# A hybrid decoder step (RWKV-7, RG-LRU, cross-attention): TensorE's order fixed by hand in the RWKV chain and the LRU stage, units reordered, keys scaled per token

## The chip, the core and the metric

The kernel runs on one core of one Trainium2 chip. The metric is the device time of one execution, in microseconds; less is better. The core has five engines with an instruction stream each: TensorE (PE; its weight loads are shown apart as PEld), VectorE (DVE), ScalarE (ACT), GpSimd (POOL) and SyncE (SP, which issues most DMAs). They wait for each other by semaphores, and each runs its own stream in order.

## The reference

One layer, for a prompt of 512 tokens and for 8 samples of 8 tokens (576 tokens in all), width 1024:

```python
xn = rmsnorm(x, g_norm)
u, za, xb, zb, q, zc, gates = split_in(xn @ w_in)      # 1024 x 11392
oa, ... = rwkv7_branch(u, za, ...)     # 16 heads of 64: s = s*w + sa (kk*a)^T + v k^T ; o = s r
ob, ... = rglru_branch(xb, zb, ...)    # conv of 4, two block gates, h = a*h + b
oc = cross_attn(q, zc, mem_k, mem_v)   # 4 heads of 256, 256 memory rows
g_a, g_b, g_c = split(sigmoid(gates))
merged = g_a * (oa @ w_br_a) + g_b * (ob @ w_br_b) + g_c * (oc @ w_br_c)
y = x + merged @ w_out                 # then a last rmsnorm
```

In the RWKV branch the key direction `kk` is normalized per token and head: `kk * rsqrt(sum(kk*kk) + eps)`. The samples bring states and memory keys and values of their own; the prompt starts from zero states and computes its keys and values (`kv`).

## The kernel before

**The stream.** All large projections are cut into units of 128 output columns (class `Stream`, `step` at line 330). Operands are split in two parts (`hi` and `lo`, type fp32r), so a step is three products (hi*xh, hi*xl, lo*xh), each in two halves of 288 tokens: six matmuls on the whole 128x128 array, all recorded at line 355. Eight steps make a unit. Its weights (512 KB) are fetched by SP, ScalarE makes `whi` (line 280) and VectorE makes `wlo` (line 281), one unit ahead; at the end of a unit the evacuation (`use`) is queued. `st.go(n)` writes n steps at that place of the program, `st.until(label)` all steps to the end of a unit. Units come from two lists: `first` (needed at a due place) and `fill` (spilled to DRAM until used). Names in the profile are those of the units: `u` (RWKV inputs), `za`, `zb`, `zc` (gates), `xb` (LRU input), `g` (merge gates), `q`, `kv`, `br` (branch outputs).

**Order.** The program is written with the stream's steps between the pieces of the branches. A scheduler then orders each engine's instructions by what is ready in its estimate, so single stream matmuls and small products are mixed more finely than they are written.

**Stages.** Start and norms (to 62 us), memory keys and values with attention (`attention`, line 660, to 223), RWKV (`rwkv_phase`, line 802, to 884), the last `zb` units (to 936), the LRU stage beside the projections `br2` and `br0` (`lru_phase`, line 468, to 1065), `br1` (to 1119), output projection and norm (`final`).

**An RWKV group.** Four groups of two pairs of heads (`o0`, `o1`), in chunks of 64 tokens; a ninth chunk holds the samples. `prep_a`, `prep_b`, `prep_c` make decays and keys; the products `m` (line 990) of keys and reads are masked and, on VectorE, multiplied by the reciprocal key norm `rsv`, which lies per partition there (`M`, line 996). The same factor goes into the transposed keys (`BKn`, line 981). `invert` (line 1000) sends 32x32 blocks of `M` through DRAM (`d<-M`, `X<-d`) and solves 72 unit triangles by substitution on VectorE (lines 1016, 1018); `invert2` (line 1035) fetches the result, and TensorE forms the other blocks: `z` (line 1041) and `w` (line 1050) on 32x32 tiles of the array, in two halves of nine, each result copied by ScalarE (lines 1045, 1054). `solved` (line 1082) then applies the inverses (`U`, `W` on 64x64 tiles). The chain (line 1123) goes over eight chunks; in each, `A` (line 1128, whole array) multiplies by the state `sbd`, VectorE adds it to `UV` (line 1121), then `dS` (line 1137) and `A` (line 1113) run on 128x64 tiles, and the new state is made by POOL (line 1130) and VectorE (line 1145). `sample_a`, `sample_b`, `sample_c` handle the samples' states inside the chain (`s0t`, `A8` at line 1189 on 128x32 tiles, `dSs`, `s1t`). The stream between these is what `st.go(2)` and `st.go(4)` put there.

**The LRU stage.** For each of eight column blocks: `conv` (ScalarE and VectorE), `gates` (products `pg`, line 516; tanh and exponentials on ScalarE; scaling by `c4` on VectorE, line 521), `scan` (POOL makes `be`, lines 543 and 544; VectorE scans at line 546 and multiplies by the gate), and `split` (line 590) into the operand of the last projections (`oh`, `ol`). The sum over branches (`merged`) is on POOL for the middle branch (line 452).

Of the kernel before, what the change touches and what calls it, by code (L numbers as in the profile page):

```python
# [18 lines left out]
P = 128  # L19
D = 1024  # L20
KC = 8
# [25 lines left out]
class Kern:  # L47
    def __init__(self, ctx, tc, ins, outs):
# [7 lines left out]
        self.dq = 0  # L56

# [4 lines left out]
    def transpose(self, out, in_, rows):  # L62

        self.nc.tensor.transpose(out, in_, self.ident[:rows, :rows])  # L64
# [151 lines left out]
    def softplus(self):  # L216
# [9 lines left out]
        nc.vector.tensor_scalar(self.c4, self.c4, -4.0, None, op0=ALU.mult)  # L226

# [77 lines left out]
class Stream:  # L305
# [24 lines left out]
    def step(self):  # L330
# [22 lines left out]
        for q, (a, b) in enumerate(((hi, xh), (hi, xl), (lo, xh))):  # L353
            for o, t0, m in parts:
                nc.tensor.matmul(self.ps[:, o:o + m], a[:, k, :], b[:, k, t0:t0 + m],  # L355
                                 start=(k == 0 and q == 0), stop=(k == KC - 1 and q == 2))
# [35 lines left out]
def spill_units(K, pool):  # L392
# [38 lines left out]
    us = [Unit(w, C_G + D * b + P * j, x, gate(K.gd[b, j]), f"g{b}{j}") for b in (2, 0, 1) for j in range(KC)]  # L431
    us += [Unit(w, C_ZC + P * j, x, silu2(K.ocz[j], K.ocd[j]), f"zc{j}") for j in range(KC)]
    us += [Unit(w, C_XB + P * j, x, conv_in(j), f"xb{j}") for j in range(KC)]
    us += [Unit(w, C_ZB + P * j, x, silu2(K.zbd[j]), f"zb{j}") for j in range(KC)]
    return us


def branch_units(K, pool, b, w, oh, ol, place, out=None):
# [3 lines left out]
    def mk(j):  # L442
        def use(pb):
# [7 lines left out]
            if place == "mid":  # L451
                nc.gpsimd.tensor_add(m, m, t)
# [15 lines left out]
def lru_phase(K, o2, then):  # L468
# [4 lines left out]
    with tc.tile_pool(name="lruc", bufs=1, reuse_waits="tile") as lc, tc.tile_pool(name="lru", bufs=2, reuse_waits="tile") as lp:  # L473
# [9 lines left out]
        ohl = []  # L483
# [21 lines left out]
        def gates(j):  # L505
            if j % 4 == 0:
                quad[j // 4] = lp.tile([P, 4, N], F32, tag="args", name="args")
# [3 lines left out]
            for q, bh in enumerate((K.bah, K.bxh)):  # L511
                g = lp.tile([P, N], F32, tag=f"g{q}", name=f"g{q}")
                for s in range(2):
                    pg = K.psb(f"pg{q}")[:, 0:HN]
                    cs = slice(HN * s, HN * s + HN)
                    nc.tensor.matmul(pg, wbd[q][:, j, :], xc[:, cs], start=True, stop=True)
# [3 lines left out]
            c4 = K.c4[:, j:j + 1]  # L520
            nc.vector.tensor_scalar(gr, gr, c4, c4, op0=ALU.mult, op1=ALU.add)
# [3 lines left out]
            nc.scalar.activation(ap_, gr[:, 0:TP], AF.Exp)  # L525
            nc.scalar.activation(as_[:, :, 1:9], smp(gr), AF.Exp)
            th = lp.tile([P, AE], F32, tag="th", name="th")[:, 0:N]
            nc.scalar.activation(th, gr, AF.Tanh, scale=-1.0)
            nc.scalar.activation(gr, gr, AF.Exp, scale=2.0)
            nc.vector.scalar_tensor_tensor(ar, gr, 1.0, th, op0=ALU.add, op1=ALU.mult)  # L530
            gx = lp.tile([P, N], F32, tag="gx", name="gx", bufs=4)
# [3 lines left out]
        def scan(j):  # L535
# [7 lines left out]
            nc.gpsimd.tensor_mul(bp_, ar[:, 0:TP], gx[:, 0:TP])  # L543
            nc.gpsimd.tensor_mul(bs_[:, :, 1:9], smp(ar), smp(gx))
# [5 lines left out]
            o = lp.tile([P, N], F32, tag="g0", name="lo")  # L550
            nc.vector.scalar_tensor_tensor(o[:, 0:TP], hp_, 0.5, z2[:, 0:TP], op0=ALU.mult, op1=ALU.mult)
# [956 lines left out]
```

## Time and profile before

| | |
|---|---|
| median of 3 runs | 1182.16 us (1181.98 to 1182.41) |
| the profiled execution | 1184.47 us |
| its span in the trace | 1182.7 us |
| mean granted TensorE clock | 0.992 |
| busy share PE, DVE, ACT, POOL | 97%, 60%, 44%, 16% |
| the chain that ended last | PE 79%, DVE 7%, ACT 5%, issue 3%, DMA 3%, POOL 2% |
| HBM | read 120.82 MB, written 29.01 MB, 127 GB/s over the span |

Matmuls overlap in the trace: a stream matmul is recorded with about 0.30 us, and the next one starts 0.13 us after it. So a busy share of TensorE says little about how close together its matmuls are; the chain in order of time, whose pieces are merged from start to start, says more. A row of the timeline merges neighbours of one kind (x2, x8); in square brackets stands idle time before it, and what ended it. A float32 product of the program appears as two records.

### The profile page before, as it was taken

The page shows a single profiled execution, that of the slowest core. Times are in us where ns is not written, and L with a number is a line of the kernel's source. Part 1 is how long each engine was busy: PE and PEld are TensorE (multiplying, and loading weights), DVE is VectorE, ACT ScalarE, POOL GpSimd, SP SyncE. Part 2 cuts the span into 40 slices and gives each one's busy share as a digit, 9 for nine tenths or more (in the row PEclk, how much of TensorE's full clock was granted, in tenths as well). Part 3 has the DMA queues.
Part 4 walks back from the last instruction along what each step waited for, and adds up shares of the span by engine and source line. Part 5 has one row for each costly group of instructions (what it writes and reads, how often), then busy time and mean ns, then how long its engine had stood idle before and what let it go on. Part 6 is the DMA issues. An engine that isn't in the chain of part 4 may idle for free.

```text
span 1182.7 us, 25731 instructions
## 1 busy us (share of the span) xinstructions
PE 1145.4 (97%) x10567; PEld 1068.8 (90%) x10567; DVE 713.2 (60%) x1436; ACT 517.3 (44%) x1004; POOL 184.3 (16%) x311
## 2 busy tenths in 40 slices
PE   6999999999999999999999999999999999979997
PEld 4998877899998898988989989999889999979997
DVE  5345655238764687835788457874455386975633
ACT  5444544337324374243752336532444266442333
POOL 3010001010003210022100130101211012570031
PEclk9999999999999999999999999999999999998999
DMA  4447685522452233532233522345337665348412
GB/s 140 130 145 233 211 254 189 162 81 66 107 140 73 65 93 82 142 89 70 78 92 120 145 73 65 106 125 149 85 90 232 203 195 170 104 115 261 117 45 81
DMA packets 220623, 151.50 MB, mean 128 GB/s; under 512 B 52640, under 2 KB 196106, under 8 KB 220506
## 3 DMA queue, kind: packets, MB, share of 16 engines
q1 hardware_dynamic: 217242, 146.87, 42.1%
q10 hardware_dynamic: 3264, 2.99, 0.9%
q8 instruction: 83, 1.36, 0.5%
q14 instruction: 34, 0.28, 0.1%
HBM read 120.82 MB, written 29.01 MB: 127 GB/s over the span
## 4 chain that ended last, share of the span: by engine, by line
PE 79%; DVE 7%; ACT 5%; issue 3%; DMA 3%; POOL 2%; SPq 0%; DVEq 0%; ACTq 0%; POOLq 0%
PE u L355 13%; PE g L355 12%; PE br L355 9%; PE xb L355 4%; PE zc L355 4%; PE za L355 4%; PE fo L1349 4%; PE q L355 4%; PE zb L355 3%; PE kv L355 2%; PE m L990 1%; PE dS L1137 1%; DVE wlo L281 1%; DMA wraw<-in_w_mem_kv 1%; PE skt L64 1%
## 5 line engine op out<-in xcount | busy, mean ns | idle before, releaser
L280 ACT CAST whi<-wraw 128x1024 fp32r<-128x1024 f32 x129 | 135.4, 1050 | 292.6 <-PE g L355 90.7
L281 DVE TENSOR_TENSOR wlo<-wraw,whi 128x1024 fp32r<-128x1024 f32 x128 | 158.9, 1241 | 127.5 <-ACT whi L280 126.7
L355 PE MATMUL u<-xh,whi 128*128 128x288 f32 x400 | 92.2, 305 | 0.0
L355 PE MATMUL br<-oh,wlo 128*128 128x288 f32 x384 | 84.4, 302 | 4.4 <-DVE wlo L281 4.3
L355 PE MATMUL u<-xl,whi 128*128 128x288 f32 x400 | 88.6, 300 | 0.0
L355 PE MATMUL u<-xh,wlo 128*128 128x288 f32 x400 | 88.6, 299 | 0.0
L355 PE MATMUL br<-oh,whi 128*128 128x288 f32 x384 | 85.4, 305 | 3.0 <-ACT oh L592 2.9
L355 PE MATMUL g<-xh,whi 128*128 128x288 f32 x384 | 86.6, 304 | 0.0
L355 PE MATMUL g<-xh,wlo 128*128 128x288 f32 x384 | 84.7, 300 | 0.0
L355 PE MATMUL g<-xl,whi 128*128 128x288 f32 x384 | 84.4, 301 | 0.0
L355 PE MATMUL br<-ol,whi 128*128 128x288 f32 x384 | 84.2, 301 | 0.0
L355 PEld LDWEIGHTS u<-xh,whi 128*128 128x128 f32 x400 | 65.1, 188 | 5.5 <-issue 4.1
L355 PEld LDWEIGHTS br<-oh,wlo 128*128 128x128 f32 x384 | 63.5, 194 | 5.6 <-DVE wlo L281 5.6
L355 PEld LDWEIGHTS br<-oh,whi 128*128 128x128 f32 x384 | 63.7, 193 | 4.3 <-ACT oh L592 3.4
L355 PEld LDWEIGHTS u<-xl,whi 128*128 128x128 f32 x400 | 64.7, 188 | 2.0 <-issue 1.4
L355 PEld LDWEIGHTS u<-xh,wlo 128*128 128x128 f32 x400 | 64.7, 188 | 0.9 <-issue 0.2
L355 PEld LDWEIGHTS g<-xh,whi 128*128 128x128 f32 x384 | 62.3, 190 | 3.2 <-issue 3.1
L355 PEld LDWEIGHTS g<-xh,wlo 128*128 128x128 f32 x384 | 62.7, 190 | 1.2 <-issue 1.2
L355 PEld LDWEIGHTS br<-ol,whi 128*128 128x128 f32 x384 | 63.4, 193 | 0.1
L355 PEld LDWEIGHTS g<-xl,whi 128*128 128x128 f32 x384 | 62.4, 190 | 1.1 <-issue 1.1
L1016 DVE TENSOR_TENSOR Xt<-X 72x30 f32<-72x30 f32 (+14 forms) x120 | 39.3, 328 | 11.4 <-DMA X<-d 7.8
L1349 PE MATMUL fo<-wol,oh 128*128 128x256 f32 (+1 forms) x160 | 45.0, 282 | 0.0
(386 smaller groups left out, 2894.3 us busy)
## 6 DMA issues: line engine op xcount, KB each, us to landing
wraw<-in_w_in SPq DMA_DIRECT2D x89, 512.0 KB
wraw<-in_w_mem_kv SPq DMA_DIRECT2D x16, 512.0 KB
kn<-in_cache_mem_k SPq DMA_DIRECT2D x16, 512.0 KB
kn<-in_cache_mem_v SPq DMA_DIRECT2D x16, 512.0 KB
gd<-flt SPq DMA_DIRECT2D x24, 288.0 KB
gtt<-gd SPq DMA_DIRECT2D x24, 288.0 KB
wraw<-in_w_br_c SPq DMA_DIRECT2D x8, 512.0 KB
wraw<-in_w_br_a SPq DMA_DIRECT2D x8, 512.0 KB
```

Source lines behind the costliest of these rows:

```text
L64: self.nc.tensor.transpose(out, in_, self.ident[:rows, :rows])
L280: nc.scalar.copy(hi, raw)
L281: eng.tensor_sub(lo, raw, hi.bitcast(F32))
L355: nc.tensor.matmul(self.ps[:, o:o + m], a[:, k, :], b[:, k, t0:t0 + m], start=(k == 0 and q == 0), stop=(k == KC - 1 and q == 2))
L990: nc.tensor.matmul(pms[h][64 * w:64 * w + 64, P * (c - c0):P * (c - c0) + P], BK[64 * h:64 * h + 64, c, w, :], ZR[64 * h:64 * h + 64, c].r ...
L1016: nc.vector.tensor_mul(tv, X[:, 0:s, s:s + 1].to_broadcast([NQ, s, m]), X[:, s:s + 1, s + 1:].to_broadcast([NQ, s, m]))
L1137: nc.tensor.matmul(pS[hs, C * o.q:C * o.q + C], o.BKn[:, c, hs], o.UV[:, c, hs], start=True, stop=True, tile_position=(0, 64 * h))
L1349: nc.tensor.matmul(pos[t][:r, :W], a[:, k, t * P:t * P + r], b[:, k, :], start=(k == 0 and q == 0), stop=(k == KC - 1 and q == 2))
```

## The change

It has six parts.

1. **Order fixed by hand.** All matmuls go through a helper `mm` (line 71 of the changed kernel), transposes through line 65. While `K.pin` is set, their order on TensorE is that of the program. It is set through the chain of each RWKV group and through the LRU stage. A chain step is now: A with the state, `s0t` or `s1t` if any, two stream steps (one in the last group), then `dS`, `A` and the samples' products on tiles, then four (three) stream steps.
2. **Inversion.** 38 in place of 37 steps before `invert2`, and the first M block is sent to DRAM per pair of heads as soon as it is made (`products`); `invert` only loads, `substitute` solves.
3. **Keys scaled by channel row, not by partition.** The reciprocal norms are made in `prep_a`, written to DRAM transposed (1152 elements of 4 bytes a pair), and read back to all partitions into `sq`. The keys are multiplied by it before the products, so that the mask is one multiplication for four chunks, and the transposed keys are plainly copied by ScalarE.
4. **Attention.** The samples' scores of the second group are written beside the values of the first (one PSUM bank, same 128x32 tiles), loads are issued close to their use, and more stream steps lie between.
5. **Fill order.** `zb`, 16 gates, `xb`, 4 gates, `zc`, and the last 4 gates, in place of gates, `zc`, `xb`, `zb`.
6. **LRU stage.** It starts when `zc7` is done, beside the last four gate units; the gate products are spread, scans of the first half come before the rest's gates, the operand `oh`/`ol` is made later; `c4` becomes scale and bias of ScalarE's activations; `be` and the middle sum of `merged` go from POOL to VectorE. The last states are written out after `br11`.

Cut to its core:

```diff
+    def mm(self, *a, **kw):
+
+        ins = self.nc.tensor.matmul(*a, **kw)
+        if self.pin:
+            self.tc.keep_in_program_order(ins)
+        return ins
...
-    us = [Unit(w, C_G + D * b + P * j, x, gate(K.gd[b, j]), f"g{b}{j}") for b in (2, 0, 1) for j in range(KC)]
...
+    return zb + g[:16] + xb + g[16:-4] + zc + g[-4:]
...
             if place == "mid":
-                nc.gpsimd.tensor_add(m, m, t)
+                nc.vector.tensor_add(m, m, t)
...
-            nc.vector.tensor_scalar(gr, gr, c4, c4, op0=ALU.mult, op1=ALU.add)
...
-            nc.scalar.activation(ap_, gr[:, 0:TP], AF.Exp)
+            nc.scalar.activation(ap_, gr[:, 0:TP], AF.Exp, scale=c4, bias=c4)
...
-            nc.gpsimd.tensor_mul(bp_, ar[:, 0:TP], gx[:, 0:TP])
-            nc.gpsimd.tensor_mul(bs_[:, :, 1:9], smp(ar), smp(gx))
+            nc.vector.tensor_mul(bp_, ar[:, 0:TP], gx[:, 0:TP])
+            nc.vector.tensor_mul(bs_[:, :, 1:9], smp(ar), smp(gx))
...
+        K.pin = True
+        conv(0)
+        st.go(8)
+        conv(1)
+        st.go(6)
+        gates(0)
+        conv(2)
+        st.go(5)
+        gates(1)
+        st.until("g17")
+        oa, then = merge()
...
+            rvf = rv.rearrange("p h c -> p (h c)")
+            nc.vector.reciprocal(rvf, rvf)
+            d4 = dr.tile([18, C], F32, tag="d4", name="d4")
+            nc.sync.dma_start(d4.rearrange("x t -> t x"), rvf)
+            d4h = d4.rearrange("(h c) t -> h (c t)", h=2)
+            for h in range(2):
+                nc.sync.dma_start(sq[64 * h:64 * h + 64, :], d4h[h:h + 1, :].to_broadcast([64, N]))
...
-            nc.vector.scalar_tensor_tensor(sq, ta, 1.0, zn, op0=ALU.add, op1=ALU.mult)
-            nc.vector.tensor_mul(BK[:, :, zs, :], chk(sq), chk(o.pinv))
+            nc.vector.tensor_mul(sq, sq, o.pinv)
+            nc.vector.scalar_tensor_tensor(BK[:, :, zs, :], chk(ta), 1.0, chk(zn), op0=ALU.add, op1=ALU.mult)
+            nc.vector.tensor_mul(BK[:, :, zs, :], BK[:, :, zs, :], chk(sq))
...
+                for h in range(2):
+                    nc.vector.tensor_mul(M1.rearrange("p (c h) m -> p c h m", h=2)[:, c0:c0 + n, h, :],
+                                         pms[h][:, 0:P * n].rearrange("p (c m) -> p c m", m=P),
+                                         maskq[q][c0 == 8].unsqueeze(1).to_broadcast([P, n, P]))
...
-            st.go(37)
+            st.go(38)
             invert2(prs)
...
+            K.pin = True
             for c in range(8):
-                chain(prs, c)
-                if c in (1, 4):
-                    sample_a(prs[c // 4])
-                if c in (2, 5):
-                    sample_b(prs[c // 4])
-                if c in (3, 6):
-                    sample_c(prs[c // 4])
+                chain(prs, c, (2, 4) if g + 1 < NG else (1, 3), fulls.get(c, none), tileds.get(c, none))
+            K.pin = False
```

On TensorE in a chain step of the first group, before (u are stream units, M the two pairs' products; x2 counts neighbours of one kind):

```order
L1128 MATMUL A<-sbd_2475,ZR 128x128 x2
L355 MATMUL u_4497<-xl,whi 128x288 x2
L355 MATMUL u_4497<-xh,wlo 128x288 x2
L1137 MATMUL dS<-UV,BKn 64x64 x2
L355 MATMUL u_4598<-xh,whi 128x288
L1137 MATMUL dS<-UV,BKn 64x64 x2
L1113 MATMUL A<-UV,M_3281 64x64
L1113 MATMUL A<-UV,M_3428 64x64
```

And in such a step of the changed kernel:

```order
L71 MATMUL A<-sbd_2645,ZR 128x128 x2
L71 MATMUL u_4443<-xh,whi 128x288 x2
L71 MATMUL u_4443<-xl,whi 128x288 x2
L71 MATMUL u_4443<-xh,wlo 128x288 x2
L71 MATMUL u_4443<-xh,whi 128x288 x2
L71 MATMUL u_4443<-xl,whi 128x288 x2
L71 MATMUL u_4443<-xh,wlo 128x288 x2
L71 MATMUL dS<-UV,BKn 64x64 x4
L71 MATMUL A<-UV,M_3412 64x64
L71 MATMUL A<-UV,M_3534 64x64
```

Twelve stream matmuls now stand between A with the state and dS, and none stands among the tile products.

On TensorE at the inversion of the first group, before (the first z, of the first pair, stands 13 rows of stream ahead of this):

```order
L355 MATMUL u_4256<-xl,whi 128x288 x2
L1041 MATMUL z_3972<-xz,M_3428 32x32 x9
L1050 MATMUL w_3993<-M_3281,xz 32x32 x9
L355 MATMUL u_4256<-xh,wlo 128x288 x2
L355 MATMUL u_4256<-xh,whi 128x288 x2
L355 MATMUL u_4256<-xl,whi 128x288 x2
```

And in the changed kernel:

```order
L71 MATMUL g_4091<-xh,wlo 128x288 x2
L71 MATMUL z_4149<-xz,M_3412 32x32 x9
L71 MATMUL z_4150<-xz,M_3534 32x32 x9
L71 MATMUL w_4171<-M_3412,xz 32x32 x9
L71 MATMUL w_4172<-M_3534,xz 32x32 x9
L71 MATMUL z_4193<-xz,M_3412 32x32
```

The stream matmuls between z and w have gone ahead of all of them; the two pairs' second z and w follow, and then U.

On VectorE near the end of the LRU stage, before (he is the scan, lo its gated result, ol the operand's low part, br a branch projection's result):

```order
L546 SCALAR_TENSOR_TENSOR he<-ae,be 128x584 x2
L593 TENSOR_TENSOR ol<-lo,oh 128x576
L450 SCALAR_TENSOR_TENSOR gtt<-gtt,br_12562 128x576
L551 SCALAR_TENSOR_TENSOR lo<-he,z_12649 128x512
L552 SCALAR_TENSOR_TENSOR lo<-he,z_12649 128x64
L551 SCALAR_TENSOR_TENSOR lo<-he,z_12704 128x512
L552 SCALAR_TENSOR_TENSOR lo<-he,z_12704 128x64
L281 TENSOR_TENSOR wlo<-wraw,whi 128x1024
```

And in the changed kernel:

```order
L557 TENSOR_TENSOR be<-args,gx 128x512
L558 TENSOR_TENSOR be<-args,gx 128x8x8
L464 SCALAR_TENSOR_TENSOR gtt<-gtt,br_12334 128x576
L560 SCALAR_TENSOR_TENSOR he<-ae,be 128x584
L466 TENSOR_TENSOR merged<-merged,gtt 128x576
L564 SCALAR_TENSOR_TENSOR gx<-he,z_12359 128x512
L565 SCALAR_TENSOR_TENSOR gx<-he,z_12359 128x64
L557 TENSOR_TENSOR be<-args,gx 128x512
L558 TENSOR_TENSOR be<-args,gx 128x8x8
L294 TENSOR_TENSOR wlo<-wraw,whi 128x1024
```

The products be and the sum into merged now stand in VectorE's stream, and one scan lies between two wlo where two did.

More of the change, by code (lines that the diff above doesn't have):

```diff
@@ L465, in load_split, with lru_phase @@
         split(nc, oh[:, k, :], ol[:, k, :], t)
-def lru_phase(K, o2, then):
+def lru_phase(K, o2, merge, operand):
     nc, tc, i, pv = K.nc, K.tc, K.i, K.pv
@@ L506, in gates @@
             if j % 4 == 0:
[L507 removed]
+                quad[j // 4] = lp.tile([P, 4, N], F32, tag="args", name="args", bufs=1)
             ar = args[j] = quad[j // 4][:, j % 4, :]
@@ L557, in roots, with lru_out @@
             nc.scalar.activation(q4, q4, AF.Sqrt, scale=0.25)
-        for j in range(4):
-            conv(j)
-            st.go(9 if j else 13)
+        K.pin = True
[9 more added lines that the diff above has]
+        oa, then = merge()
+        conv(3)
+        st.go(4)
+        gates(2)
+        st.go(5)
+        gates(3)
+        st.go(5)
+        roots(0)
+        for j in range(4):
+            scan(j)
+            st.go(5)
+        then()
+        conv(4)
+        for j in (4, 5, 6):
+            conv(j + 1)
+            st.go(6)
             gates(j)
-            if j == 3:
-                then()
+        st.until("br27")
+        ohl = operand(o2)
+        for j in range(4):
+            split(nc, ohl[0][:, j, :], ohl[1][:, j, :], keep[j][1])
             st.go(3)
-        st.until("br27")
-        ohl = [o2.tile([P, KC, N], F32R, tag=tag, name=tag) for tag in ("oh", "ol")]
-        roots(0)
-        for j in range(4, KC):
-            conv(j)
-            st.go(4)
-            scan(j - 4)
-            st.go(3)
-            gates(j)
-            st.go(3)
+        gates(7)
         roots(4)
         for j in range(4, KC):
+            st.go(5)
             scan(j)
-            st.go(9)
+            split(nc, ohl[0][:, j, :], ohl[1][:, j, :], keep[j][1])
+        K.pin = False
+    return ohl, lambda: lru_out(K, lo_st, cv_st)
+def lru_out(K, lo_st, cv_st):
     lf = lo_st.rearrange("p a b -> p (a b)")
@@ L818, in rwkv_phase @@
         pe = [pe2[:, q, :] for q in range(G)]
-        rsv = [rc.tile([P, NCH, 2], F32, name=f"rsv{q}") for q in range(G)]
+        rsv = [rc.tile([P, 2, NCH], F32, name=f"rsv{q}") for q in range(G)]
         onat = rc.tile([P, NCH, P], F32, name="onat")
@@ L929, in prep_b @@
             zs = 1 - q
-            pr_ = K.psb("rs")
-            for c in range(NCH):
-                nc.tensor.matmul(pr_[br:br + 64, 2 * c:2 * c + 2], o.sq[:, C * c:C * c + C], K.bones2, start=True, stop=True,
-                                 tile_position=(0, br))
-            rvf = rsv[q][br:br + 64].rearrange("p c h -> p (c h)")
-            nc.vector.tensor_scalar(rvf, pr_[br:br + 64, 0:18], -2.0, -2.0 * L2_EPS, op0=ALU.mult, op1=ALU.add)
-            nc.vector.reciprocal(rvf, rvf)
             BK = o.BK = rg.tile([P, NCH, 2, C], F32, tag="BK", name="BK")
@@ L1282, in rwkv_phase @@
                 st.go(3)
-            UV2[0] = rg.tile([P, G, NCH, P], F32, tag="UV", name="UV", bufs=1)
+                scaled(o)
+                products(o)
+                st.go(3)
+            X = invert()
             for o in prs:
                 prep_c(o)
-                st.go(6)
-            invert(prs)
+                st.go(3)
+            substitute(prs, X)
             direct(prs)
```

336 lines of the change are left out of this document (190 added, 146 removed).

## The prediction

> **What bounds the kernel now.** I read the page's first part, then the busy time by stage, the chain in order of time through one RWKV group, and TensorE's timeline where the stages show it idle.
>
> ```profile
> PE 1145.4 (97%) x10567; PEld 1068.8 (90%) x10567; DVE 713.2 (60%) x1436; ACT 517.3 (44%) x1004; POOL 184.3 (16%) x311
> 223.00:884.00 661.00, 654.08 (x6909) 610.86 (x6908) 427.22 (x955) 286.96 (x589) 91.49 (x153) 1.00 0.35 98
> 936.00:1004.00 68.00, 68.00 (x480) 65.89 (x479) 49.12 (x69) 42.56 (x67) 10.99 (x26) 1.00 0.61 185
> 1004.00:1065.00 61.00, 53.85 (x361) 50.62 (x359) 51.81 (x58) 28.02 (x45) 41.26 (x45) 0.97 0.38 107
> 1065.00:1119.00 54.00, 53.60 (x382) 53.60 (x383) 29.52 (x35) 15.62 (x20) 2.33 (x1) 0.94 0.63 197
> ```
>
> The columns of the stage rows are the stretch, its length, the busy time of PE, PEld, DVE, ACT and POOL, the granted clock, the DMA share and GB/s. TensorE sets the time nearly everywhere, and only the stage from 1004 has much idle time on it. So the change can win in two ways: cheaper TensorE work at the same busy share, or less idle time.
>
> A busy TensorE is not one at its best. The chain in order of time (start, length, instruction and count) shows it:
>
> ```profile
> 311.58 36.80 PE g L355 x276
> 379.00 0.38 PE dS L1137 x8
> 379.38 0.23 PE A L1113 x8
> 387.89 0.27 PE dS L1137 x4
> 388.16 0.33 PE u L355
> 388.49 0.27 PE dS L1137 x4
> 388.75 0.23 PE A L1113 x8
> ```
>
> A stream matmul on the whole array takes 36.80/276 = 133 ns from start to start. The eight dS and eight A on array tiles take 0.38 + 0.23 = 0.61 us where they stand together. With one stream matmul among the dS the same takes 0.27 + 0.33 + 0.27 + 0.23 = 1.10 us, of which 0.13 is that matmul's own work: 0.36 us lost for two more changes of tile shape, 0.18 each. Where longer runs meet, a change costs less:
>
> ```profile
> 352.29 0.43 PE L355 MATMUL u<-xh,whi 128*128 128x288 f32 x2
> 352.56 0.42 PE L355 MATMUL u<-xl,whi 128*128 128x288 f32 x2
> 352.91 0.66 PE L1041 MATMUL z<-xz,M 32*32 32x32 f32 x15
> ```
>
> Two stream matmuls take 0.27 us from start to start, but 0.35 when z on 32x32 tiles is next: 0.08 us for the change.
>
> The idle time from 1004 on, in TensorE's timeline and then VectorE's:
>
> ```profile
> 1048.66 0.43 PE L355 MATMUL br<-oh,wlo 128*128 128x288 f32 x2
> 1052.01 0.51 PE L355 MATMUL br<-oh,whi 128*128 128x288 f32 x2 [2.92 <-ACT oh L592]
> 1054.99 0.69 PE L355 MATMUL br<-oh,whi 128*128 128x288 f32 x2
> 1065.40 0.85 PE L355 MATMUL br<-oh,wlo 128*128 128x288 f32 x2 [2.97 <-DVE wlo L281]
> 1068.00:1072.00 4.00, 4.00 (x21) 4.00 (x21) 0.48 (x1) 0.15 (x1) 1.76 (x1) 0.59 1.02 363
> 1057.63 2.58 DVE L546 TENSOR_TENSOR_SCAN he<-ae,be 128x584 f32<-128x584 f32 x1 [1.39 <-POOL be L544]
> 1064.14 1.21 DVE L281 TENSOR_TENSOR wlo<-wraw,whi 128x1024 fp32r<-128x1024 f32 x1
> ```
>
> The scan stands in VectorE's queue until POOL has multiplied be, and the weights' low parts (wlo) stand behind scans and output products; TensorE runs dry for 2.92 and 2.97 us. After each, pairs of matmuls take 0.69 us in place of 0.42, and the granted clock is 0.59 in 1068 to 1072. By count the two stages hold 361 and 382 matmuls, 743 x 0.133 = 98.8 us of work in 115 us: 16 us lost.
>
> **The change part by part.** *Tile shapes.* The matrix work stays the same. In the order of TensorE's instructions neighbours of different tile shape fall from 332 to 177: in the attention stage from 52 to 28, per RWKV group in the chain from 34 to 39 down to 18, in the inversion from 10 to 2, the rest in the prep. That is 155 fewer, at 0.08 to 0.18 us each: 12 to 28 us. Many removed pairs enclosed one to four stream matmuls, many others more, so I take 0.12: **-18.6 us**.
>
> *LRU stage.* It is begun four stream units earlier (4 x 48 x 0.133 = 25 us), and the operand of the last projections is due later. What VectorE does there:
>
> ```profile
> L281 DVE TENSOR_TENSOR wlo<-wraw,whi 128x1024 fp32r<-128x1024 f32 x128 | 158.9, 1241 | 127.5 <-ACT whi L280 126.7
> L521 DVE TENSOR_SCALAR g<-g,c 128x576 f32<-128x576 f32 x8 | 5.7, 715 | 3.2 <-ACT g L517 3.2
> L543 POOL TENSOR_TENSOR be<-args,gx 128x512 f32<-128x512 f32 x8 | 12.0, 1495 | 9.9 <-ACT args L557 9.9
> L452 POOL TENSOR_TENSOR merged<-merged,gtt 128x576 f32<-128x576 f32 x8 | 15.9, 1983 | 13.7 <-DVE gtt L450 13.7
> L454 DVE TENSOR_TENSOR gtt<-gtt,merged 128x576 f32<-128x576 f32 x8 | 6.0, 753 | 0.1
> ```
>
> The be product and the merging sum move from POOL to VectorE (8 x 0.75 each by the row of L454, 1.5 more for be's second instruction: +13.5 us), the scaling of L521 goes into ScalarE's activations (-5.7). In 936 to 1065 VectorE had 49.1 + 51.8 = 101 us in 129; it gets some 109 plus four units' own work (4 x 2, a wlo and an evacuation each), 117 us in 129 - 16 + 25 = 138: 85%. That is tight but no bound, and the scan no longer waits for another engine. Of the 16 us I take 11 back: **-11 us**; bounds -16 (no wait left) and +8 (VectorE late as before with 8 us more work). The first gate products, now pinned in order, may wait for VectorE's convolution: +1.
>
> *Inversion.* z and w now stand back to back with nothing between, and each waits for the other's copy:
>
> ```profile
> 348.64 0.68 PE z L1041 x18
> L1045 ACT COPY xz<-z 32x288 f32<-32x288 f32 x16 | 6.2, 391 | 12.9 <-PE z L1041 12.5
> L1054 ACT COPY M<-w 32x288 f32<-32x288 f32 x16 | 6.2, 388 | 12.7 <-PE w L1050 12.3
> 353.69 0.39 ACT L1045 COPY xz<-z 32x288 f32<-32x288 f32 x1 [3.26 <-PE z L1041]
> ```
>
> The copy starts at 353.69, about 0.1 us behind z's last product, and takes 0.39. First w: 0.55 us of waiting. Second w: four copies of 0.39 stand before it on ScalarE against 0.68 us of z, 0.6 more. U: 0.3. Stream matmuls between hid nearly all of this before. So 1.25 us in each of four groups: **+5 us**, bounds 0 (other work of TensorE put between) and +7 (0.6 at each of three places).
>
> *The substitution's cover.* VectorE solves the triangles while TensorE runs stream units; z needs the result, which goes through DRAM.
>
> ```profile
> 303.35 0.37 PE m L990 x4
> L1011 SPq DMA_DIRECT2D X<-d x1: 307/307/307, 311.3 to 311.3; - x1
> L1016 DVE TENSOR_TENSOR Xt<-X x30: 186/347/405, 314.4 to 340.5; 72x30 f32<-72x30 f32 x2, 72x58 f32<-72x58 f32 x2, 72x84 f32<-72x84 f32 x2, 72x108 f32<-72x108 f32 x2
> L1032 SPq DMA_DIRECT2D M<-d x4: 321/490/496, 344.4 to 346.9; - x4
> ```
>
> From the last product m at 303.4 to the last return from DRAM at 346.9, with the 3.1 us that X took from issue (311.3) to use (314.4), it is 46.6 us. In the changed order 282 stream matmuls (37.6 us) and some 9.6 us of other work stand between, 47.2 us; before it was 49.5 (z at 352.91). The masking before it becomes shorter, but one more wlo may be caught in VectorE's queue. I take half a microsecond of waiting per group: **+2 us**, bounds 0 and +6.
>
> *Chain.* In a step TensorE multiplies by the state (A), VectorE adds (UV), and dS uses that sum. Between stand now always 12 stream matmuls, 1.6 us, 6 in the last group.
>
> ```profile
> L1121 DVE TENSOR_TENSOR UV<-A,UV 64x128 f32<-64x128 f32 x64 | 18.5, 289 | 28.1 <-PE A L1128 26.5 <-PE A L1189 0.2
> 402.62 0.34 PE L1137 MATMUL dS<-UV,BKn 128*64 128x64 f32 x4 [0.24 <-DVE UV L1121]
> ```
>
> Two additions of 0.29 and the way there and back need about 1.3 us. Where a wlo of 1.24 us has just begun on VectorE, dS waits, and since TensorE's order is pinned everything queued behind it, stream included, waits too. One wlo comes per unit of 6.4 us, so this meets about every fifth of 28 additions, by some 0.2 us more than before: +1 us, bounds 0 and +7 (0.24 at each).
>
> *Prep.* The factors from rs now go to DRAM as 4-byte elements and come back to all partitions, both on SP's queue, where the stream's weight loads stand behind their waits. The nearest row is the way of M to X: store issued by 307.0 (the last of its kind in group 0), load issued 311.3, used 314.4, 7.4 us. TensorE has 12.3 us of work in the order between rs and the first product that needs the scaled keys, and VectorE wants some 3 us of it for scaling and reciprocal: 10.5 of 12.3. The Trainium skill's "DMA: Bandwidth & Descriptors" (section "Anatomy of one DMA") puts most of a transfer's fixed 2 us into the write's receipt; the estimate from that for two transfers is 4 us, the row says 7.4, and I go by the row. VectorE's masks get cheaper:
>
> ```profile
> L996 DVE SCALAR_TENSOR_TENSOR M<-m,rsv,mask 128x128 f32<-128x128 f32 x72 | 18.9, 342 | 0.0
> L981 DVE TENSOR_TENSOR BKn<-bkt,rsv 128x512 f32<-128x512 f32 x16 | 10.9, 686 | 2.0 <-PE bkt L64 1.2 <-PE vt L64 0.7
> ```
>
> 18 of 342 ns become four of 512 columns (686) and two small ones, some 3 us less per pair of heads, and the 686s of L981 go to ScalarE, which is 43% busy in 223 to 884. Sum 0, bounds -3 (the waits for M are gone) and +28 (below).
>
> *Attention.* Keys and values of the samples are loaded some 4 us ahead, less than before; in 62 to 223 TensorE was idle for 3.8 us at most:
>
> ```profile
> 62.00:223.00 161.00, 157.21 (x1252) 133.35 (x1252) 79.31 (x162) 70.57 (x135) 8.94 (x21) 0.99 0.67 209
> ```
>
> One wait fewer or one more: 0, bounds -3 and +4. The units' new order changes no work.
>
> **Sum:** -18.6 - 11 + 1 + 5 + 2 + 1 = -20.6 us against the profiled execution of 1184.47 us (span 1182.7): 1163.9. The median of the runs is 2.3 us below that execution, so 1161.6, in round numbers **1162 us**.
>
> **The rivals.**
>
> 1. *Slower: SP's queue in the prep.* If the way through DRAM with its 1152 4-byte elements takes 5 us more than the nearest row, or the second pair's store waits behind the first pair's return (2 x 7.4 = 14.8 against 12.3), TensorE waits at m, and the weight loads behind on SP come late. At 5 us per group that is 20 us, and after such a wait the clock is at half for 3 to 6 us, as at 1054 and 1066: twice 0.13 us per pair, some 2 us, so 28 in all, and the time is 1162 + 28 = 1190. It decides from about 4 us per group on (20.6/4, less the half clock). Against it: the margin of 1.8 us, and the second pair's store is issued a pair's preparation later, not with the first. Chance 8%.
> 2. *VectorE bounds the LRU stage.* The 13.5 us more on it come in the same queue as wlo, and pinned gate products stop the stream. Then the 11 us are not won: 1173; with +8 it is 1181. For it: 85% in a queue served in order. Against it: no POOL step in the scan's path. Chance 20%, most of it at 1173.
> 3. *The change of shape costs little that isn't lost again.* In the RWKV groups TensorE's saving (131 changes x 0.12 = 15.7 us) would turn into waits for the substitution, which grows no shorter: 1162 + 14 = 1176. For it: that path has under 1 us of margin. Against it: only some 2.5 us per group of the saving lie in that stretch. Chance 10%.
> 4. *Hardly a new wait.* With shape changes at 0.14, all of the 16 us and new waits of 3 us in place of 9: 1182.2 - 21.7 - 16 + 3 = 1147. For it: the copies at the inversion may overlap more than I count. Against it: VectorE at 85%. Chance 9%.
> 5. *Short waits lower the clock.* The stage 223 to 884 has a granted clock of 1.00 in spite of short waits, such as the 0.24 above; the two long ones of 2.9 us lowered it. If 0.6 us three times in a row at the inversion did so too, half clock for some 3.4 us would cost 1.7 us in each group: 1169. The Trainium skill ("TensorE: Matmul & The Clock Gate", "A second HAM failure mode: psum-queue depth-cycling") tells of frequent micro-idles with such an effect, and its Part 1 gives about 3.4 us for the idle window. The trace agrees with the window, and shows nothing of the other. Chance 4%.
>
> **How the numbers follow.** The forecast has 49%, with a range of its own from 1155 to 1169 (its terms at two thirds of their bounds). Range 1149 to 1178: it takes in rivals 2, 3 and 5 but for the worst of 2, and nearly all above 1147 of 4; left out are rival 1 and the ends, about 16%. About 0.2%, 2.4 us, is what a measurement of this kernel can tell from no change. Slower by more: rival 1 and a little of 2, 0.09. Within: 0.03. Faster: 0.88.
>
> **What would show it.** Right: shape changes at some 180 in TensorE's records, chain steps with dS x4 and A x8 in one piece of about 0.6 us; no wait over 1 us and clock 1.00 after 936; z to U some 1.3 us longer than its matmuls. Wrong: waits of some us at m behind the broadcast of the factors (rival 1), waits for wlo or the gate products from 936 on (rival 2), a wait at z over 2 us in each group (rival 3), a clock under 1.00 behind the inversion (rival 5). If the time falls by less than 10 us with fewer changes of shape, their price is what I got wrong.

## The result, and the profile after

| | before | changed |
|---|---|---|
| median | 1182.29 us (1181.98 to 1184.73, 4 runs) | 1212.74 us (1211.04 to 1216.58, 4 runs) |
| ratio | | 1.0257, 95% interval 1.0229 to 1.0285 |
| span of the profiled execution | 1182.7 us | 1210.7 us |
| mean granted TensorE clock | 0.992 | 0.966 |

The change makes the kernel 30 us slower; 1162 was forecast. The first line of the changed kernel's page:

```profile
PE 1135.9 (94%) x10567; PEld 1077.3 (89%) x10567; DVE 687.6 (57%) x1342; ACT 533.3 (44%) x1028; POOL 154.2 (13%) x285
```

TensorE is busy for 9.5 us less, and stands idle for more (74.8 us in place of 37.3). Where, the stage rows say: the attention stage, one prep (from the first rs to R), and the two parts of the LRU stage, then the same prep of the kernel before.

```profile
67.70:230.80 163.10, 159.09 (x1328) 141.24 (x1329) 82.16 (x160) 69.07 (x130) 8.59 (x19) 1.00 0.64 204
448.80:497.50 48.70, 41.01 (x390) 38.23 (x390) 26.96 (x49) 25.36 (x55) 3.94 (x3) 0.86 0.34 77
944.00:1007.00 63.00, 61.61 (x435) 59.51 (x433) 45.74 (x66) 41.29 (x61) 11.34 (x28) 1.00 0.64 202
1007.00:1092.00 85.00, 78.09 (x538) 75.20 (x537) 60.73 (x86) 42.79 (x60) 9.17 (x16) 0.94 0.55 167
```

```profile
432.10:461.10 29.00, 28.36 (x325) 25.85 (x324) 26.77 (x66) 14.95 (x32) 0.00 (x0) 1.00 0.31 91
```

The prep has 157 stream matmuls in place of 108, which explains 6.5 of the 19.7 us; the rest is 7 us more of idle TensorE and half clock (the mean granted clock is 0.86). The chain in order of time shows the two waits of the first group's prep (start, length, what):

```profile
290.87 11.30 DMA d<-rsv
...
302.24 0.48 SPq L995
...
304.04 9.51 DMA d<-rsv
...
314.12 3.59 DMA sq<-d
...
319.23 0.68 DVE BK L1010
...
320.04 3.95 PE m L71 x63
```

The store of the factors, 4.5 KB in 4-byte elements, takes 11.30 us from issue to landing, the second one 9.51, and the loads 3.59. The second pair's store goes out at 304.04 only, behind the first pair's loads on SP. In all four groups the first pair's store takes 11.2 to 12.3 us from issue to the load behind it, the second pair's 7.8 to 9.6. TensorE's timeline beside it:

```profile
301.63 0.68 PE L71 MATMUL g<-xh,whi 128*128 128x288 f32 x2
...
308.57 4.10 PE L71 MATMUL m<-ZR,BK 64*64 64x128 f32 x60 [5.33 <-DVE BK L1010]
...
320.04 4.41 PE L71 MATMUL m<-ZR,BK 64*64 64x128 f32 x68 [2.61 <-DVE BK L1010]
```

The products m wait 5.33 and 2.61 us for the scaled keys, and the stream ahead of the first wait already runs at half clock (0.68 us a pair in place of 0.42). No long wait stands ahead of that: TensorE waits 0.82 and 0.72 us before the two pairs' products rs, which have only two columns each. What lowered the clock there was not tried. In all, SP waited 61 us for these stores (the queue's own waits; total, times, longest):

```profile
SPq L995 <- DMA d<-rsv: 61.0, 7, 9.6
```

The chain step is what was forecast, dS and A in one piece of 0.61 us and no wait before dS:

```profile
386.39 0.38 PE dS L71 x8
386.78 0.23 PE A L71 x8
...
388.80 1.60 PE u L71 x12
390.40 0.44 PE A L71 x4
390.85 1.60 PE u L71 x12
392.45 0.38 PE dS L71 x8
```

And in the LRU stage a pinned gate product waits for the convolution, which stands behind seven splits in VectorE's queue; the work behind the wait runs at half clock for 5.7 us. TensorE's timeline:

```profile
1014.19 4.21 PE L71 MATMUL pg<-xc,wbd 128*128 128x288 f32 x8 [6.91 <-DVE xc L515]
1017.79 1.10 PE L71 MATMUL br<-oh,whi 128*128 128x288 f32 x2
```

VectorE's timeline beside it: five splits, the convolution's first steps, two more splits, and then its last step, which ends at 1014.14 (1013.39 + 0.75), just ahead of the product. The last two splits themselves waited 0.73 us for ScalarE's `oh`, and ScalarE before that 2.19 us for a load of `oxl`; so the queue's order is not the only delay.

```profile
1005.53 3.43 DVE L626 TENSOR_TENSOR ol<-oxl,oh 128x576 fp32r<-128x576 f32 x5
1008.88 2.35 DVE L513 SCALAR_TENSOR_TENSOR cva<-xe,par,cva 128x600 f32<-128x600 f32 x3
1011.96 1.51 DVE L626 TENSOR_TENSOR ol<-oxl,oh 128x576 fp32r<-128x576 f32 x2 [0.73 <-ACT oh L625]
1013.39 0.75 DVE L515 SCALAR_TENSOR_TENSOR xc<-xe,par,cva 128x512 f32<-128x512 f32 x1
```

At the inversion the clock falls as well. It is at half in three of the four groups, for 6.8, 3.4, 6.8 and 0 us. A stage row behind the first group's z and w, with a granted clock of 0.50, and the products U in TensorE's timeline:

```profile
374.00:378.00 4.00, 4.00 (x80) 3.94 (x77) 0.48 (x1) 1.36 (x3) 0.00 (x0) 0.50 0.76 204
374.89 3.61 PE L71 MATMUL U<-r,M 64*64 64x64 f32 x66
```

In the kernel before, the same products took 2.14 us:

```profile
359.17 2.14 PE L1092 MATMUL U<-r,M 64*64 64x64 f32 x66
```

To compare stages in which different amounts of stream stand, I take from each stage's length its 288-column stream matmuls at 0.1333 us (and the 256-column ones at 0.1197). What is left is small products, shape changes, waits and half clock. Stages are cut at TensorE's first rs, R, z and dS of each group, at the state's transpose (Sf) and at the first br and fo; sums over four groups, us:

| net of stream | before | changed | e1 | e3 | e5 | e9 | e12 |
|---|---|---|---|---|---|---|---|
| start and attention | 114.4 | 107.7 | 108.6 | 109.2 | 113.0 | 114.3 | 112.4 |
| prep (Sf or first rs to R) | 71.8 | 119.6 | 79.0 | 88.0 | 71.8 | 71.9 | 72.5 |
| R to z | 21.6 | 21.6 | 40.9 | 21.6 | 21.6 | 51.0 | 21.9 |
| inversion (z to dS) | 35.2 | 40.6 | 50.9 | 40.7 | 37.5 | 48.9 | 36.2 |
| chain (dS to Sf) | 80.1 | 63.9 | 62.7 | 62.9 | 69.1 | 65.4 | 71.9 |
| LRU and projections | 31.7 | 29.8 | 29.9 | 28.4 | 29.4 | 30.4 | 21.8 |
| end | 56.8 | 56.5 | 56.5 | 56.5 | 56.8 | 56.8 | 56.5 |

Changed less before is +28.1 by this table, and 28.0 by the spans. The prep alone is +47.8: TensorE stands idle in it for 32.0 us more than before, and works for 39.8 us at half clock, which costs about half of that, 19.9 us (an estimate). The two make 51.9, so its other work became a little cheaper.

### The profile page after: what moved, and what is told of

It reads as the page before. It is cut to its first block, busy times and chain, and to the rows that moved or that the text cites. A ratio compares the mean times of both kernels' runs of the same rounds, so it can differ in the third digit from the quotient of the medians.

```text
span 1210.7 us, 25638 instructions
## 1 busy us (share of the span) xinstructions
PE 1135.9 (94%) x10567; PEld 1077.3 (89%) x10567; DVE 687.6 (57%) x1342; ACT 533.3 (44%) x1028; POOL 154.2 (13%) x285
## 4 chain that ended last, share of the span: by engine, by line
PE 72%; DMA 12%; DVE 6%; issue 4%; ACT 4%; SPq 1%; POOL 0%; DVEq 0%; ACTq 0%; POOLq 0%
PE u L71 13%; PE g L71 11%; PE br L71 11%; DMA d<-rsv 4%; PE xb L71 4%; PE fo L71 4%; PE q L71 3%; PE zb L71 3%; PE kv L71 2%; PE A L71 2%; PE zc L71 2%; DMA sq<-d 1%; PE pg L71 1%; PE skt L65 1%; DMA kn<-in_cache_mem_k 1%
## 5 line engine op out<-in xcount | busy, mean ns | idle before, releaser
L71 PE MATMUL u<-xh,whi 128*128 128x288 f32 x400 | 89.6, 306 | 0.0
L71 PE MATMUL u<-xl,whi 128*128 128x288 f32 x400 | 85.9, 297 | 0.0
L71 PE MATMUL u<-xh,wlo 128*128 128x288 f32 x400 | 85.8, 296 | 0.0
L71 PE MATMUL m<-ZR,BK 64*64 64x128 f32 x576 | 33.5, 344 | 30.8 <-DVE BK L1010 22.5
L71 PEld LDWEIGHTS m<-ZR,BK 64*64 64x64 f32 x576 | 25.9, 173 | 37.3 <-DVE BK L1010 20.9
```

The costliest lines, as they stand in the source:

```text
L71: ins = self.nc.tensor.matmul(*a, **kw)
```

## The experiments

Times stand beside runs of the kernel before on the same chip (1182.5 to 1184.1 us); ratios are to it, with 95% intervals.

**e1: the key norms stay in SBUF.** Part 3 undone, the rest as changed.

```diff
-            nc.sync.dma_start(d4.rearrange("x t -> t x"), rvf)
...
-                    nc.vector.tensor_mul(M1.rearrange("p (c h) m -> p c h m", h=2)[:, c0:c0 + n, h, :],
...
+                        nc.vector.scalar_tensor_tensor(M1[:, 2 * c + h, :], pms[h][:, P * (c - c0):P * (c - c0) + P],
+                                                       rsv[q][:, c, h:h + 1], maskq[q][c == 8],
```

> The changed kernel with its third part undone: the reciprocal key norms stay in SBUF per partition, multiply each block of M and the transposed keys as before, and nothing goes through DRAM for them. Theory 1 (the way of the factors through DRAM on SP's queue is what the change loses; by stage it costs some 13.4 us in each of four groups, 54 us): 1212.7 - 54 plus some waits of m on VectorE's slower masks (about 1 us per group) = 1160 to 1168, faster than the kernel before. Theory 2 (the fixed order and the closer inversion lose it, and the wait at m only stands in for waits that would come at z): the waits move to z and the time stays above 1190.

Measured: 1200.9 us, ratio 1.0145 (1.0115 to 1.0174). The prep falls from 119.6 to 79.0, as Theory 1 has it. But of these 40.6 us 19.3 come back between R and z, as waits for the substitution, and 10.3 in the inversion behind them, where the clock is at half for 46 us in all; so the time is in Theory 2's range. TensorE's timeline, second group:

```profile
523.20 1.16 PE L71 MATMUL z<-xz,M 32*32 32x32 f32 x18 [5.31 <-DMA xz<-d]
525.73 1.00 PE L71 MATMUL z<-xz,M 32*32 32x32 f32 x15 [1.36 <-DMA xz<-d]
```

With the norms off the way the scheduler fills TensorE with stream ahead of the last products: 238 stream matmuls are left between them and z in place of 282 (groups two to four).

**e2: the norms by a product with ones, on TensorE.**

```diff
+                K.mm(pn, K.bones.bitcast(F32), sq[:, cs], start=True, stop=True)
+                nc.vector.tensor_scalar(sq[:, cs], pn, -2.0, -2.0 * L2_EPS, op0=ALU.mult, op1=ALU.add)
+            nc.vector.reciprocal(sq, sq)
```

> The changed kernel, but the norms come to all partitions by a product with a block of ones on TensorE (4 products of 288 columns a pair in place of 18 small ones), and VectorE takes the reciprocal of 576 columns; the keys are still scaled before the products. Theory 1: no DRAM way, so 1155 to 1165; if the reciprocal of 576 columns is dear on VectorE (the row of 18 columns takes 0.26 us, which does not tell), up to 4 us per pair more, and m waits for it. Theory 2: above 1190.

Measured: 1195.97 us, ratio 1.0116 (1.0101 to 1.0131). That is Theory 2's range: the cover is 235 matmuls here, and z waits 5.6 us in the first group and 1.4 to 2.0 in the others. VectorE pays for the reciprocal, by its group row:

```profile
L986 DVE RECIPROCAL sq<-sq 128x576 f32<-128x576 f32 x8 | 30.0, 3750 | 0.1
```

**e3: the store in rows of 72 bytes.**

```diff
-            d4 = dr.tile([18, C], F32, tag="d4", name="d4")
-            nc.sync.dma_start(d4.rearrange("x t -> t x"), rvf)
-            d4h = d4.rearrange("(h c) t -> h (c t)", h=2)
+            d4 = dr.tile([C, 18], F32, tag="d4", name="d4")
+            nc.sync.dma_start(d4, rvf)
+            d4h = d4.rearrange("(h t) x -> h (t x)", h=2)
```

> The changed kernel, but the store of the factors writes rows of 72 bytes as they lie, not 4-byte elements transposed; the loads are the same. The factors then stand at the wrong tokens, so the result of the RWKV branch is another. Theory 3 (the 4-byte elements make the store slow, 9.5 to 11.3 us from issue to landing against 3.6 us for the loads): the store takes 2 to 4 us, the first pair's wait at m (5.4 us) goes, and the time is 1165 to 1180. Theory 4 (any store and load through DRAM on SP takes this long there, because SP waits behind other things): the store stays above 8 us and the time within 5 us of 1212.

Measured: 1180.07 us, ratio 0.9979 (0.9962 to 0.9997), 33 us less than the changed kernel (1.0257) for the same bytes on the same queue. The DMAs of these tiles in the second group (issues on SP; first and last start):

```profile
L995 SPq DMA_DIRECT2D sq<-d x4: 444/588/611, 444.5 to 452.9; - x4
...
L992 SPq DMA_DIRECT2D d<-rsv x2: 452/456/461, 441.1 to 450.6; - x2
```

The first load goes out 3.4 us behind its store (441.1 to 444.5), where it was 12.3 in this group; over all eight pairs it is 1.7 to 3.4 us, where it was 7.8 to 12.3, and the second pair's store is no longer held up behind the first pair's loads. Theory 3 holds, with the time at the upper end of its range: cutting the same bytes into 1152 elements instead of 64 rows is the price. What is left of the prep's loss (88.0 against 71.8) is 12.6 us more of idle TensorE and 17.1 us at half clock; in this group m waits 3.31 us for M.

**e4: the loads issued later,** so that on SP they don't stand between the two stores.

```diff
-            for h in range(2):
-                nc.sync.dma_start(sq[64 * h:64 * h + 64, :], d4h[h:h + 1, :].to_broadcast([64, N]))
```

(the two lines stand in prep_b instead)

> The changed kernel, but the two loads of a pair are issued at the start of the key stage, not right behind the store, so that on SP the second pair's store is not queued behind the first pair's loads. The store itself stays as it is. Theory 3 (store length): the first pair's wait of some 5 us stays, only the second pair's falls: 1195 to 1207. Theory 5 (SP's order is the main thing): the second pair's wait and the half clock behind it go, and most of the loss with them: 1175 to 1190.

Measured: 1213.84 us, ratio 1.0267 (1.0252 to 1.0282), no gain; both theories expected one. But the edit did not reach what it was meant to change. SP's timeline in the first group:

```profile
303.32 0.45 SPq L1003 DMA_DIRECT2D sq<-d  x1
303.81 0.62 SPq L992 DMA_DIRECT2D d<-rsv  x1
```

The first pair's loads (line 1003) still stand ahead of the second pair's store (line 992), in all four groups. So this run tests no other order on SP, and says nothing for or against Theory 5: what the queue's order alone is worth stays open.

**e5: the kernel before with the new chain.** Only the order of the chain's small products and transposes is changed and pinned; the stream is not pinned.

```diff
-                if c in (1, 4):
-                    sample_a(prs[c // 4])
...
+            K.pin = True
             for c in range(8):
+                chain(prs, c, (2, 4), fulls.get(c, none), tileds.get(c, none))
+            K.pin = False
```

> The kernel before with one part of the change alone: the chain of the RWKV groups in the new order and pinned (two and four stream steps in all four groups, as before). Shape changes fall from 332 to 286, the chain's from 34-39 to 24-26 a group. Theory 1 (a shape change in the chain costs 0.12 to 0.18 us, and the fixed order adds no waits): 46 x 0.12 to 0.18 = 5.5 to 8.3 us, 1174.5 to 1177.5. Theory 2 (the fixed order itself loses, by stream held up behind dS): no faster than 1182.

Measured: 1171.64 us, ratio 0.9893 (0.9873 to 0.9914). The chain falls by 11.0 us net for 46 fewer shape changes, 0.24 us each, more than the 0.18 that I took as the upper bound. This figure includes whatever else the new order saved in a step.

**e6: e1 with ten more stream steps before z.**

```diff
-            st.go(38)
+            st.go(48)
```

> The first experiment (key norms kept in SBUF) with 48 in place of 38 stream steps between the substitution's start and z, so that some 298 in place of 235 stream matmuls cover it. Theory 1 (what the first experiment lost against 1165 was the wait at z of 5 us a group and half clock behind it, since the scheduler had moved stream ahead of the products): the wait at z goes, 19 us in the stage up to z and some 8 us in the inversion behind it come back, 1170 to 1178. Theory 2: the wait shows up at another place, and the time stays above 1190.

Measured: 1201.72 us, ratio 1.0153 (1.0138 to 1.0168), no gain in total, so Theory 2's range. R to z falls from 40.9 to 23.1 and the inversion from 50.9 to 42.8, 26 us, as expected; but the 40 steps are missing later, and the first pinned gate product of the LRU stage stands without stream ahead of it:

```profile
954.14 5.51 PE L71 MATMUL pg<-xc,wbd 128*128 128x288 f32 x16 [25.16 <-DVE xc L517]
```

Why the first convolution comes so late there was not tried.

**e7: the norms spread by small products, the rest as changed.**

```diff
+                        K.mm(pn[64 * h:64 * h + 64, C * (c - c0):C * (c - c0) + C],
+                             rv[:, h, c:c + 1].to_broadcast([C, C]), K.ident[br:br + 64, br:br + 64], start=True, stop=True,
+                             tile_position=(br, 64 * h))
```

> The changed kernel with one thing replaced: the reciprocal norms are spread over the channels by 18 small products a pair on TensorE (from SBUF, by an identity), not by a store and loads through DRAM. The keys are scaled before the products as in the change, the cover of z stays at 282 stream matmuls. It adds some 1.1 us of TensorE a pair (as the U products, 36 records in 1.1 us) and 19 shape changes. Theory 1 (the way through DRAM is what the change loses): the prep falls from 113 to some 65 us net of stream, 1160 to 1172. Theory 2 (the wait only moves to z): above 1185.

Measured: 1191.62 us, ratio 1.0092 (1.0053 to 1.013). The cover stays at 282 and z does not wait. But the products now come while VectorE still waits for POOL with the group before (VectorE's timeline, its work for the old group, then M):

```profile
459.77 3.15 DVE L1329 SCALAR_TENSOR_TENSOR oT<-oT,tza 128x576 f32<-128x576 f32 x2 [0.70 <-POOL oT L1327]
462.85 2.27 DVE L1053 TENSOR_TENSOR M<-m,mask 128x512 f32<-128x512 f32 x5
```

TensorE's timeline beside it:

```profile
463.58 0.69 PE L71 MATMUL m<-ZR,BK 64*64 64x128 f32 x4 [3.03 <-DVE M L1053]
```

So neither theory had it: without the DRAM way the change's prep still costs some 25 us more than before's (89.9 + 7.2 against 71.8). Of these, 12.1 us are idle TensorE, most of it at m; 10.1 are the added products themselves (288 records); and some 3.4 are what 6.8 us at half clock cost (an estimate).

**e8: the same, with the fifth convolution ahead of the splits.**

```diff
+        conv(4)
         then()
-        conv(4)
```

> The same, and in the LRU stage the fifth convolution is written ahead of the splitting of the RWKV output's operand, not behind it. Theory: the pinned gate product that waits 7 us for it, at half clock for some us behind, then comes in time: 7 to 9 us faster than the kernel next to it. Rival: the splits then come late and the projection of the RWKV output waits instead: the same time.

Measured: 1190.74 us, ratio 1.007 (1.0047 to 1.0092): by time not to be told from e7. In the trace the gate product's wait falls from 7.2 to 1.9 us and the stage from the first br by 4.9 us, but the second group's prep was 2.8 us longer.

**e9: e5 with the stream pinned too.**

```diff
-                nc.tensor.matmul(self.ps[:, o:o + m], a[:, k, :], b[:, k, t0:t0 + m],
+                K.mm(self.ps[:, o:o + m], a[:, k, :], b[:, k, t0:t0 + m],
```

> The fifth experiment (the kernel before with the new chain) with the stream's own matmuls pinned in the chain as well, as the change does it. The scheduler can then no longer bring nine steps of the chain's stream forward: 244 stream matmuls cover z in place of 300, and none stands between z and w. Theory 6 (pinning the stream takes the substitution's cover away): a wait of about 5 to 7 us at z in each group, half clock for some us behind it (2 to 3 us), and 1.3 us at the inversion, against 15 fewer shape changes a group (2 us): 1171.6 + 4 x 7 = 1193 to 1203. Theory 1 (pinning costs nothing): 1165 to 1172.

Measured: 1211.29 us, ratio 1.0233 (1.0213 to 1.0254), 40 us more than e5 for this line. Theory 6 holds, and is dearer than I wrote. TensorE at z in the four groups:

```profile
346.50 2.08 PE L1052 MATMUL z<-xz,M 32*32 32x32 f32 x33 [5.51 <-DMA xz<-d]
...
508.09 2.22 PE L1052 MATMUL z<-xz,M 32*32 32x32 f32 x33 [5.83 <-DMA xz<-d]
...
672.61 1.17 PE L1052 MATMUL z<-xz,M 32*32 32x32 f32 x18 [9.12 <-DMA xz<-d]
...
837.22 2.28 PE L1052 MATMUL z<-xz,M 32*32 32x32 f32 x33 [8.60 <-DMA xz<-d]
```

29 us of waits, and behind each the inversion at a lower clock, 0.69 of full over these 11 us of the first group (the stage row):

```profile
341.00:352.00 11.00, 5.02 (x115) 4.85 (x116) 0.81 (x1) 2.34 (x6) 1.40 (x1) 0.69 0.55 123
```

The two stages grow by 40.8 us net.

**e10: the changed kernel with the prep of before,** 46 stream steps before z and one less per chunk in the chain.

```diff
-            st.go(38)
+            st.go(46)
...
-                chain(prs, c, (2, 4) if g + 1 < NG else (1, 3), fulls.get(c, none), tileds.get(c, none))
+                chain(prs, c, (2, 3) if g + 1 < NG else (1, 3), fulls.get(c, none), tileds.get(c, none))
```

> The changed kernel with the second and third part undone: prep, products and key norms in the code and order of the kernel before (no DRAM way of the factors). The stream before z is 46 steps (298 matmuls of cover) and one step less per chunk in the chain. So chain, attention, unit order and LRU stage are those of the change. Theory 1, by stages net of stream from the traces: 59 in the prep as before, 22, inversion some 40, chain 64, and the gains of attention (-7) and LRU stage (-7, less 5 at its start): 1182 - 16 - 7 - 2 + 5 = 1158 to 1166. Theory 2 (the loss is in the fixed order or in the other parts): above 1182.

Measured: 1197.33 us, ratio 1.0109 (1.0085 to 1.0133). That is far from Theory 1's 1158 to 1166. The prep is 72.5 again, but with a pinned stream the steps are short at other places: z of the last group waits 5.7 us, the first gate product 10.7 and the fifth 6.9, and the inversions run at half clock for 27 us.

**e11: the same with the fifth convolution ahead.**

> The same with the fifth convolution of the LRU stage ahead of the operand's splitting, as in the eighth experiment, where that stage became 5 us shorter by the trace: 4 to 7 us less than the kernel next to it, 1152 to 1161.

Measured: 1192.27 us, ratio 1.0076 (1.0055 to 1.0097). The stage from the first br falls from 25.2 to 20.2 us; the intervals of e10 and e11 overlap, and the time is 31 us above the range expected.

**e12: prep of before, stream not pinned, fifth convolution ahead.** `step` calls `nc.tensor.matmul` again; all else as in e11, with 37 and (2, 4) steps.

> The changed kernel with prep, products and key norms as before (no DRAM way), the stream's matmuls not pinned (only the small products of chain and LRU stage and the transposes are), and the fifth convolution ahead of the operand's splitting. The order gives 300 to 314 stream matmuls of cover before z, as in the kernel before, and 274 shape changes. Theory (pinned stream and DRAM way are the two losses, chain, attention and LRU stage the gains): the fifth experiment's 1171.6, less 7 for attention and 5 to 9 for the LRU stage, 1155 to 1163. Rival (the new LRU stage loses at its start, as in the experiments with 48 and 46 steps, where a gate product waited 11 and 25 us): 1170 or more.

Measured: 1162.91 us, ratio 0.984 (0.9821 to 0.9859), faster than both kernels and in the theory's range. The gains add up: chain -8.2, LRU -9.9, start and attention -2.0 (in place of -6.7, which was not looked into), and little lost at prep, z or the inversion. In the last stage rows of it, the LRU stage with br2 and br0 has TensorE busy for 142 of 145 us at full clock, with VectorE at 73%:

```profile
910.00:1055.00 145.00, 142.04 (x1008) 137.77 (x1007) 105.35 (x151) 81.18 (x116) 18.46 (x42) 1.00 0.64 192
```

**e13: the changed kernel with only the stream unpinned.**

> The changed kernel with one thing undone: the stream's matmuls are not pinned. The DRAM way of the factors stays. The order gives 282 stream matmuls before z in either, and stream stands between z and w again (10 shape changes an inversion in place of 2, 221 in all). Theory 7 (in the change itself the pin costs little, since its prep is written so that 282 matmuls cover z, and the loss is the DRAM way): 1207 to 1215. Theory 6 (the pinned stream is the loss here too): below 1195.

Measured: 1209.03 us, ratio 1.0233 (1.0213 to 1.0252), its interval overlapping the changed kernel's. Theory 7 holds: in the change itself 282 matmuls cover z either way (in groups two to four), and the pin is not the main loss. By stage it does cost something. With the stream free the inversion takes 35 us in place of 40.6, without any half clock, and the LRU stage 22.6 in place of 29.8, with the gate product waiting 2.6 us in place of 6.91; the chain takes 68 in place of 63.9. The profiled execution is the fastest of five here, so these may overstate what the pin costs.

## Why the prediction was wrong, step by step

**The step that failed** is the prep, "Sum 0, bounds -3 and +28". It is +47.8 us. I took the store of M and the load of X, 7.4 us, as the nearest row for the factors' way, and put "10.5 of 12.3" beside it. One store takes 11.30 us alone, one way with its load 14.9, and both pairs in a row on SP 26.8 (290.87 to 317.71). TensorE waits for that at m, and runs at half clock around the waits. The row I used moves runs of 128 bytes; the store moves single elements. e3 shows that their size makes the time: with rows of 72 bytes the load goes out 1.7 to 3.4 us behind the store, and the kernel is 33 us faster. The Trainium skill's "DMA: Bandwidth & Descriptors" ("Specifications") gives 512 bytes as the least transfer for full rate. The runs point the same way with both sizes below that, 72 and 4 bytes, and the price is the measured one. The section of the Trainium skill that the prediction names beside this term, "Anatomy of one DMA", describes transfers issued by GpSimd, while these go out on SP; the 4 us from it was further off than the row.

**Rival 1** had the mechanism and the place, at 8%. Its price was low: 28 us against the prep's 47.8. It was held against it that "the second pair's store is issued a pair's preparation later, not with the first": it was held on SP until 304.04. What that order alone costs, the runs don't show (e4); with short stores (e3) the second pair's store is not held.

**Shape changes**, -18.6: the direction held and the size was low. The chain lost 16.2 us for 76 fewer changes, 0.21 each; e5 gives 0.24, e12 0.20 (8.2 us for 42). What else a chain step saved, such as waits hidden in these gaps, the runs don't separate.

**LRU stage**, -11: it is -1.9 together with its start. The waits of 2.9 us went, but one of 6.91 came with half clock behind it. That is rival 2's mechanism, a pinned product behind VectorE's queue, here with a late load in it; e12 brings the stage to -9.9, near the -11, with the stream free and the convolution earlier. The first gate product waited 0.29 us, not 1.

**Inversion**, +5: +5.4, but by another way, so the number is luck. The waits at w are there, shorter than forecast: 0.47 us in every group and 0.39 more in the first, and all idle time grew by 3.4 us, not 5. What rival 5 feared did occur: 16.1 us of work at half clock, about 8 us lost (an estimate). The 32 fewer shape changes there, which the sum counts under another term, made up for a part of that. Whether the short waits or the long run of small products lowered the clock is not told apart. With stream between z and w it stayed at full in the kernel before and in e13, and fell for 6.8 and 3.4 us in all in e5 and e12, against 17.1 here.

**Cover of the substitution**, +2: 0, R to z is 21.6 in both. But its margin is as thin as written: e1, e2 and e9 with 215 to 244 stream matmuls wait 1.4 to 9.1 us.

**Chain's queue**, +1: one wait of 0.97 us at a dS of the last group. **Attention**, 0 with -3 as the lower bound: -6.7, which I had not priced; it has 24 fewer shape changes, which at 0.24 would be 5.8.

Without the prep the terms give 28.1 - 47.8 = -19.7, near the -20.6 forecast, but that is partly luck: the LRU stage missed by 8 us, and the chain and the attention stage made up for it. The wrong direction came from one term, for which the traces of before held no row with elements as small.

What stays open: the change's prep without slow stores still takes 16 to 25 us more than before's (e3, e7). By amount that is waits of TensorE (12 us in either), half clock, and in e7 the added products. The waits are at m, 1.4 to 3.3 us a group (shown in the second group, behind VectorE's work for the group before), and at rs, 0.4 to 1.2 us a pair, for ScalarE. Why these come here and not in the kernel before was not tried, nor what the order of SP's queue costs by itself, nor what lowers the clock at the inversion.

## What to carry to other kernels

The time of a small DMA depended here on its pieces, not its bytes: look for a row with pieces as small, or measure one, before counting on its cover. When an order is pinned, count what the scheduler used to move under a long wait: e9 lost 40 us by pinning only the filler. Undoing a loss moves the next wait into sight, so judge each undo by its stage, not by the total alone. And look in the trace whether an edit did what it was meant to do, as with e4, before a theory falls by it.

## What the runs showed of the hardware

- A transposing store of 1152 4-byte elements took 7.8 to 12.3 us on SP's queue from issue to the load behind it; the same 4.5 KB as 64 rows of 72 bytes took 1.7 to 3.4 us (e3).
- VectorE's RECIPROCAL over 576 columns took 3750 ns (e2), 6.5 ns a column, where a TENSOR_TENSOR of that size takes about 0.75 us.
- A change of tile shape among short runs costs some 0.2 us in the chain: 0.20 to 0.24, an estimate from whole stages (8.2 us for 42, 16.2 for 76, 11.0 for 46) that includes whatever else the new order saved.
- The granted clock fell to half at the inversion with no wait over 0.5 us ahead of it (0.50 in 374 to 378), where small products on tiles stood together. It was at half for 17.1 us over the four groups there, and for 0 to 6.8 us in the runs with stream between z and w (before, e5, e12, e13).
